# Weight splits, decay factors and the last product block in another order

## The chip, the cores and the metric

The kernel runs on one core of a Trainium2 chip (trn2). A core has TensorE (PE in the profile; its weight loads are PEld), VectorE (DVE), ScalarE (ACT), GpSimd (POOL) and SyncE (SP). Each engine runs its own list of instructions in order; semaphores make one wait for another. DMA queues are fed by SP and, for transfers that add to their target, by POOL. Times are microseconds on the device; the metric is the time of one execution, the median over runs.

## The reference, cut to what matters

One layer of a decoder for 576 tokens (512 of a prompt, 64 of eight samples), D_MODEL 1024, all in float32. One RMSNorm feeds one wide projection; its columns go to a pooling mixer, to a gated linear recurrence with four heads (HGRN) and to two branch gates. Then an output projection, a SwiGLU feed-forward with D_FF 2816, and an embedding that a gate scales:

```python
h = rms_norm(x, g_mix);  z = h @ w_in                   # 4608 columns
u, zq, zf, zi, zg, ga, gb = split(z)
pool_out = multiscale_pool(u) mixed by group
f = lb + (1 - lb) * sigmoid(zf);  k = 1 - f;  v = zi;  q = silu(zq)
o, state = hgrn2_recurrence(q, k, v, log f, state)      # in chunks, decays exp(+-cumsum(log f))
ya = pool_out @ w_pool_up;  yb = (norm(o) * silu(zg)) @ w_hgrn_up
x += (sigmoid(ga) * ya + sigmoid(gb) * yb) @ w_out
h2 = rms_norm(x, g_ffn)
x += (silu(h2 @ w_ffn_gate) * (h2 @ w_ffn_up)) @ w_ffn_down
h3 = rms_norm(x, g_ple)
x += sigmoid(h3 @ w_ple_gate) * (p @ w_ple_proj)        # gate and embedding
y = rms_norm(x, g_final)
```

## The kernel before, in words

Activations lie transposed: 128 features on the partitions, 576 tokens along the free dimension, as two halves of 288. Every weight product is made from three products of rounded parts: a matrix w is split into `whi` (w rounded to fp32r) and `wlo` (the rest), activations likewise, and TensorE adds hi·hi, lo·hi and hi·lo in one PSUM bank. In `mm` these are lines 152, 154 and 156; in `prod` they are lines 869, 870 and 871. So a block of 128 output features over 1024 inputs is 48 matmuls of 128x288.

A weight unit (128x1024, 512 KB) is loaded by SP into `raw`. There are two ways to split it. `split_piece` casts on ScalarE (line 78) and subtracts on VectorE (line 79). `split_dma` casts on ScalarE (line 86 or 90), writes the negated copy on ScalarE (line 87), and then POOL issues a DMA (line 88) that reads the weight a second time from HBM and adds it to the negated copy, which gives `wlo` without VectorE. `raw` has two buffers, `whi` and `wlo` three.

The stages, in the order of the program:

- Projections for the pooling input and HGRN. `forget` and `decays` (lines 421 to 471) make, for each head, the log gate `lt`, its running sum `gt` (a scan on VectorE), some sixty small factors `fac` on POOL, and three exponentials on ScalarE (lines 468 to 470). `scaled` (line 355) is VectorE's eviction of a product from its bank (times the norm `rn`); the banks `mm` are two in this stage. `q_in`, `q_vec` and `v_vec` prepare a head; `part1` to `part5` are its small matmuls, the first of them transposes of v (line 535) and of kS (line 540).
- `up_unit` projects both branches up. It runs just ahead of the next stage.
- The branch gates, the gate, up and most of the down projection of the feed-forward go through `pair`. A pair is two blocks of 128 outputs in Winograd's form of Strassen's scheme: seven half-sized products instead of eight. Weight parts A, B, C, D of a pair come from `p_a` (A, by `split_dma`), `p_d` (D, by `split_dma`), `p_b` and `p_hi`/`p_lo` (cast and subtract, lines 850 and 854). The bank `b` of a pair starts from a copy of bank `a`, the seed (line 979). `p_all` prepares the first pair of a run while `up_unit` still multiplies, and there `p_a` of pair 1 is prepared too.
- The last quarter of the down projection, `w_dn3`: eight blocks m of 128 outputs over 512 inputs, activations `ac` (`ahh`, `ahl`), 24 matmuls each, banks ab and cd in turn. VectorE evicts each into `res` (line 1157), ScalarE rounds and squares it (lines 240, 251), VectorE makes the low part and the sum of squares (lines 241, 252).
- The gated embedding: block m is `embed(m)` (12 matmuls with `pth`/`ptl`) and a gate (48 matmuls with `h3h`/`h3l`, line 152 again), four banks `mm` of two halves. Behind gate 0 come four matmuls (lines 268, 269) of the last norm `rms`; ScalarE's square root (line 276) reads their bank and VectorE's reciprocal (line 279) makes `rn`. `ple_vec` (lines 1171 to 1176) then evicts.

The order on each engine is set by the tile framework from the order of the source, by priorities (`tc.high_priority`) and by `tc.issue_after`. From the `up_unit` stage on, PE's order is fixed by `in_order`; before that the scheduler chooses. Weights run ahead by `ahead`: when a block takes its unit, the unit two further on is split and the one four further on is loaded.

Of the kernel before, what the change touches and what calls it, by code (L numbers as in the profile page):

```python
# [20 lines left out]
KD = 8  # L21
# [7 lines left out]
def trunk(ctx: ExitStack, tc: tile.TileContext, a, o):  # L29
# [51 lines left out]
    def split_dma(raw, u, src, hi_first=False):  # L81

        n = src.shape[-1]
        raw, hi, lo = (t[:, 0:n] for t in (raw, *u))
        if hi_first:
            nc.scalar.copy(out=hi, in_=raw)
        act(lo, raw, AF.Copy, scale=-1.0)  # L87
        nc.gpsimd.dma_start(out=lo, in_=src, accum_op=ADD)  # L88
        if not hi_first:
            nc.scalar.copy(out=hi, in_=raw)  # L90
# [21 lines left out]
    seq += [a["w_dn3"][m] for m in range(KD)] + [a["w_ple_gate"][m] for m in range(KD)]  # L112
# [3 lines left out]
    def ahead(n_raw, n_split):  # L116
# [4 lines left out]
        while state["split"] < min(n_split, state["lim"]):  # L121
            i = state["split"]

            kw = dict(pl=es_pool["fp"], tag="z", bufs=2) if i >= len(seq) - 2 else {}
            if plain0 <= i < dn0 or dn0 <= i < dn0 + KD and i % 2 or up0 + 4 <= i < out0 and i % 2:
                kw["src"] = seq[i]
            splits[i] = split(raws.pop(i), seq[i].shape[-1], **kw)
            state["split"] += 1
# [225 lines left out]
    def scaled(out, pz, rn):  # L354
        tt(out=v2(out), in0=pz[:, :, 0:HT], in1=v2(rn), op=MULT)  # L355
# [80 lines left out]
    def decays(h):  # L436
# [30 lines left out]
        nc.gpsimd.tensor_copy(out=f[:, 60:68].unsqueeze(2), in_=gt[:, TP:T].rearrange("p (b t) -> p b t", t=8)[:, :, 7:8])  # L467
        act(f, f, AF.Exp)
        act(gt, lt, AF.Exp, scale=-1.0)
        act(lt, lt, AF.Exp)  # L470
        tt(out=kt, in0=kt, in1=gt, op=MULT)
# [15 lines left out]
    def q_in(h, pz):  # L487
        zq, tq = tmpa(), tmpb()
        scaled(zq, pz, rn)
        act(tq, zq, AF.Tanh, scale=0.5)  # L490
# [213 lines left out]
    for h in range(4):  # L704
# [11 lines left out]
        if h < 2:  # L716
            decays(h + 2)
            pz = unit_mm(hx)
# [247 lines left out]
    def pair(n):  # L966
# [12 lines left out]
        seed = act(q["b"], q["a"], AF.Copy)  # L979
        q.update({t: bank(t) for t in "cd"})  # L980
# [43 lines left out]
    def p_all(n):  # L1024
# [13 lines left out]
        p_a(n + 1)  # L1038
# [106 lines left out]
    us = [next_unit() for _ in range(2)]  # L1145
    pzs = [two_banks() for _ in range(2)]
    for i in range(2):
        mm(pzs[i], us[i], ac, ks=(0, 1))
    for m in range(KD):
        if m < 2:  # L1150
            pz, u = pzs[m], us[m]
            mm(pz, u, ac, ks=(2, 3))
        else:
            pz, u = two_banks(), next_unit()
            mm(pz, u, ac)
# [48 lines left out]
    NL = 4  # L1204
    for m in range(KD - NL):
        pe_ps = embed(m)
# [73 lines left out]
def lay_out(x):  # L1280
# [30 lines left out]
    d["w_dn3"] = units(wd[2304:2816], 4)  # L1311
# [32 lines left out]
```

## Time and profile before

| What | us |
|---|---|
| median of three runs | 838.72 (838.40 to 839.03) |
| the profiled execution itself | 839.74 |
| its span, first to last instruction | 837.6 |
| PE busy | 821.8 (98%) |
| VectorE, ScalarE, GpSimd busy | 605.0 (72%), 507.8 (61%), 116.7 (14%) |
| mean granted TensorE clock | 0.995 |

In the profile a row of the timeline is an instruction: start, duration, engine, line, operation, output and inputs, and in brackets how long the engine had been idle before and who released it. A matmul's duration is modelled with its pipeline (0.29 us for 128x288), while one starts every 0.13 us; so the time that PE really loses at a wait is the distance of two starts less 0.13, some 0.16 more than the bracket says.

### The profile page before, as it was taken

What the parts mean: (1) busy time and instruction counts of PE and PEld (TensorE: products, weight loads), DVE (VectorE), ACT (ScalarE), POOL (GpSimd) and SP (SyncE); (2) the same over time, 40 slices, a digit from 0 to 9 for tenths busy, and PEclk for the clock granted to TensorE, in tenths of its full rate; (3) what the DMA queues carried; (4) which work ended last, traced back from release to release, by engine and by line L of the source; (5) the groups of instructions that cost most, each with busy time, mean ns of one, the idle gap of its engine ahead of it and who ended that gap; (6) DMA issues with size and microseconds to landing.
All of it is one profiled execution on the core that took longest, in us unless ns stands there. A gap on an engine that the chain in (4) does not pass through costs nothing.

```text
span 837.6 us, 15263 instructions
## 1 busy us (share of the span) xinstructions
PE 821.8 (98%) x6092; PEld 807.2 (96%) x6092; DVE 605.0 (72%) x996; ACT 507.8 (61%) x832; POOL 116.7 (14%) x197
## 2 busy tenths in 40 slices
PE   8999999999989999999999999999999999999996
PEld 6999899999989999999999999999999999999996
DVE  7877776764877777546978778777788767577746
ACT  7356435666777666346757767665676666565434
POOL 6304120000112110001111121112111111000000
PEclk9999999999999999999999999999999999999998
DMA  7421220322757774237757686767876568464103
GB/s 238 160 83 51 76 105 29 126 105 79 186 117 178 175 176 140 76 95 155 179 123 158 133 201 175 164 142 158 210 174 159 132 154 190 96 171 126 64 1 113
DMA packets 39766, 112.48 MB, mean 134 GB/s; under 512 B 5008, under 2 KB 9104, under 8 KB 39696
## 3 DMA queue, kind: packets, MB, share of 16 engines
q1 hardware_dynamic: 24576, 74.51, 27.6%
q0 software_dynamic: 12960, 33.82, 23.7%
q10 hardware_dynamic: 2160, 3.19, 1.0%
q8 instruction: 47, 0.77, 0.4%
q14 instruction: 23, 0.19, 0.1%
HBM read 106.50 MB, written 5.00 MB: 133 GB/s over the span
## 4 chain that ended last, share of the span: by engine, by line
PE 68%; issue 17%; POOL 4%; DMA 4%; DVE 3%; ACT 2%; SPq 0%; DVEq 0%; POOLq 0%
PE mm L154 6%; PE mm L152 6%; PE mm L156 6%; PE bb L870 3%; PE bb L869 3%; PE bb L871 3%; PE ba L871 2%; PE ba L870 2%; PE ba L869 2%; DMA wlo<-in_w_ffn_up 2%; POOL dl L88 2%; POOL wlo L88 2%; PE ba L156 1%; PE ba L152 1%; PE bb L154 1%
## 5 line engine op out<-in xcount | busy, mean ns | idle before, releaser
L78 ACT CAST whi<-raw 128x1024 fp32r<-128x1024 f32 (+2 forms) x50 | 47.0, 941 | 80.4 <-PE mm L154 38.6
L154 PE MATMUL mm<-hl,whi 128*128 128x288 f32 x320 | 70.8, 301 | 1.2 <-DVE hl L241 1.2
L152 PE MATMUL mm<-hh,whi 128*128 128x288 f32 x320 | 71.0, 304 | 1.0 <-DVE ta L355 0.9
L156 PE MATMUL mm<-hh,wlo 128*128 128x288 f32 x320 | 69.5, 299 | 0.4 <-DVE wlo L79 0.4
L79 DVE TENSOR_TENSOR wlo<-raw,whi 128x1024 fp32r<-128x1024 f32 (+2 forms) x50 | 57.1, 1143 | 14.1 <-ACT whi L78 13.3
L854 DVE TENSOR_TENSOR clo<-raw,chi 128x1024 fp32r<-128x1024 f32 (+1 forms) x38 | 43.3, 1139 | 29.3 <-ACT chi L850 29.3
L152 PEld LDWEIGHTS mm<-hh,whi 128*128 128x128 f32 x320 | 52.7, 192 | 3.8 <-ACT whi L78 1.6
L154 PEld LDWEIGHTS mm<-hl,whi 128*128 128x128 f32 x320 | 52.3, 191 | 2.5 <-DVE hl L241 1.9
L156 PEld LDWEIGHTS mm<-hh,wlo 128*128 128x128 f32 x320 | 52.3, 191 | 0.7 <-DVE wlo L79 0.6
L854 DVE TENSOR_TENSOR wlo<-rb,whi 128x1024 fp32r<-128x1024 f32 (+1 forms) x38 | 43.3, 1139 | 12.2 <-ACT whi L850 12.1
L90 ACT CAST whi<-raw 128x1024 fp32r<-128x1024 f32 (+1 forms) x38 | 37.2, 978 | 22.4 <-PE ba L870 17.8
L87 ACT ACTIVATE wlo<-raw 128x1024 fp32r<-128x1024 f32 (+2 forms) x52 | 50.6, 973 | 0.0
L850 ACT CAST chi<-raw 128x1024 fp32r<-128x1024 f32 (+1 forms) x38 | 37.0, 975 | 8.9 <-DVE raw L846 8.8
L999 ACT ACTIVATE bc<-bb 128x288 f32<-128x288 f32 x38 | 15.0, 395 | 44.5 <-PE bb L871 44.5
L850 ACT CAST whi<-rb 128x1024 fp32r<-128x1024 f32 (+1 forms) x38 | 37.3, 982 | 7.1 <-PE bb L870 3.6
L90 ACT CAST dh<-rb 128x512 fp32r<-128x512 f32 (+1 forms) x38 | 22.2, 585 | 26.0 <-PE bc L870 26.0
L840 DVE TENSOR_TENSOR rb<-rb 128x512 f32<-128x512 f32 (+1 forms) x38 | 24.6, 646 | 9.0 <-ACT dl L87 4.8
L879 DVE TENSOR_TENSOR cz<-bc,p 128x288 f32<-128x288 f32 x38 | 17.3, 455 | 16.6 <-PE bc L871 16.5
L876 DVE TENSOR_TENSOR cz<-bb,p 128x288 f32<-128x288 f32 x38 | 17.3, 456 | 16.1 <-PE bb L871 11.0
L88 POOL DMA_DIRECT2D wlo<-in_w_ffn_gate x13 | 11.1, 852 | 110.8 <-ACT wlo L87 88.0
L88 POOL DMA_DIRECT2D wlo<-in_w_dn x16 | 13.5, 847 | 87.2 <-ACT wlo L87 52.4
L845 DVE TENSOR_TENSOR raw<-raw,rb 128x512 f32<-128x512 f32 (+1 forms) x38 | 24.6, 646 | 1.0 <-ACT wlo L87 0.3
(736 smaller groups left out, 3211.8 us busy)
## 6 DMA issues: line engine op xcount, KB each, us to landing
raw<-in_w_in SPq DMA_DIRECT2D x26, 512.0 KB, 3.4
raw<-in_w_ffn_gate SPq DMA_DIRECT2D x13, 512.0 KB, 3.6
raw<-in_w_ffn_up SPq DMA_DIRECT2D x13, 512.0 KB, 4.2
wlo<-in_w_ffn_gate POOLq DMA_DIRECT2D x13, 512.0 KB, 7.0
wlo<-in_w_ffn_up POOLq DMA_DIRECT2D x13, 512.0 KB, 6.9
rb<-in_w_ffn_gate SPq DMA_DIRECT2D x9, 512.0 KB, 5.5
rb<-in_w_ffn_up SPq DMA_DIRECT2D x9, 512.0 KB, 5.5
raw<-in_w_dn SPq DMA_DIRECT2D x12, 384.0 KB, 3.7
```

Source lines behind the costliest of these rows:

```text
L78: nc.scalar.copy(out=hi[:, cs], in_=raw[:, cs])
L79: tt(out=lo[:, cs], in0=raw[:, cs], in1=hi[:, cs].bitcast(F32), op=SUB)
L87: act(lo, raw, AF.Copy, scale=-1.0)
L88: nc.gpsimd.dma_start(out=lo, in_=src, accum_op=ADD)
L90: nc.scalar.copy(out=hi, in_=raw)
L152: nc.tensor.matmul(out=out[h], lhsT=wh, rhs=xh[:, h * HT:(h + 1) * HT], start=first, stop=False)
L154: nc.tensor.matmul(out=out[h], lhsT=wh, rhs=xl[:, h * HT:(h + 1) * HT], start=False, stop=False)
L156: i = nc.tensor.matmul(out=out[h], lhsT=wl, rhs=xh[:, h * HT:(h + 1) * HT], start=False, stop=last)
L850: nc.scalar.copy(out=tiles[0][:, 0:2 * q["W"]], in_=q[raw][:, 0:2 * q["W"]])
L854: tt(out=lo, in0=q[raw][:, 0:2 * q["W"]], in1=hi.bitcast(F32), op=SUB)
L869: nc.tensor.matmul(out=out, lhsT=wh, rhs=xh, start=k == 0 and not seeded, stop=False, **kw)
L870: nc.tensor.matmul(out=out, lhsT=wh, rhs=xl, start=False, stop=False, **kw)
```

## The change

Six places:

1. `split_dma`: where the cast to `whi` is not wanted first, it is now held behind the negated copy on ScalarE. Before, the scheduler took it first in some pairs.
2. `scaled` gets a higher priority on VectorE (as if it stood 80 instructions earlier).
3. `decays` is cut in two. The exponentials and the product with `kt` become `decays2`; for heads 0 and 1 they are issued inside `q_in(0)`, after `scaled`, for heads 2 and 3 right behind `decays`, and the product is held behind the latest `scaled`.
4. The A part of pair 1 in the first run is no longer made in `p_all` by negate and accumulate; `pair(0)` makes it by a cast behind its seed and a subtraction on VectorE. One accumulating DMA of 512 KB is gone.
5. `w_dn3` is laid out as four units of 128x1024, each for two blocks, in place of eight of 128x512, and all are split by cast and subtract. Before, every second one went by negate and accumulate; four accumulating DMAs of 256 KB are gone.
6. `embed(0)` and `embed(1)` are both issued ahead of gate 0.

```diff
@@ split_dma @@
-        act(lo, raw, AF.Copy, scale=-1.0)
+        neg = act(lo, raw, AF.Copy, scale=-1.0)
         nc.gpsimd.dma_start(out=lo, in_=src, accum_op=ADD)
         if not hi_first:
-            nc.scalar.copy(out=hi, in_=raw)
+            with tc.issue_after(neg.ins):
+                nc.scalar.copy(out=hi, in_=raw)
...
-    seq += [a["w_dn3"][m] for m in range(KD)] + [a["w_ple_gate"][m] for m in range(KD)]
+    seq += [a["w_dn3"][i] for i in range(KD // 2)] + [a["w_ple_gate"][m] for m in range(KD)]
...
-            if plain0 <= i < dn0 or dn0 <= i < dn0 + KD and i % 2 or up0 + 4 <= i < out0 and i % 2:
+            if plain0 <= i < dn0 or up0 + 4 <= i < out0 and i % 2:
                 kw["src"] = seq[i]
...
     def scaled(out, pz, rn):
-        tt(out=v2(out), in0=pz[:, :, 0:HT], in1=v2(rn), op=MULT)
+        with tc.high_priority(offset=80):
+            i = tt(out=v2(out), in0=pz[:, :, 0:HT], in1=v2(rn), op=MULT)
+        state["scaled"] = i.ins
...
+    def decays2(h):
+        lt, gt, kt, f = Lt[h], Gt[h], Kt[h], fac[h]
         act(f, f, AF.Exp)
         act(gt, lt, AF.Exp, scale=-1.0)
         act(lt, lt, AF.Exp)
-        tt(out=kt, in0=kt, in1=gt, op=MULT)
+        with tc.issue_after(state["scaled"]):
+            tt(out=kt, in0=kt, in1=gt, op=MULT)
@@ q_in @@
         scaled(zq, pz, rn)
+        if not h:
+            decays2(0)
+            decays2(1)
         act(tq, zq, AF.Tanh, scale=0.5)
@@ the loop over the heads @@
             decays(h + 2)
+            decays2(h + 2)
@@ pair @@
         seed = act(q["b"], q["a"], AF.Copy)
+        if n == 0:
+            with tc.issue_after(seed.ins):
+                p_hi(nq, "A", hi_lo(), "ra")
+            p_lo(nq, "A", "ra")
@@ p_all @@
         p_load(n + 1)
-        p_a(n + 1)
+        if n:
+            p_a(n + 1)
@@ the last down blocks @@
-    us = [next_unit() for _ in range(2)]
     pzs = [two_banks() for _ in range(2)]
+    u = next_unit()
     for i in range(2):
-        mm(pzs[i], us[i], ac, ks=(0, 1))
+        mm(pzs[i], u, ac, off=512 * i, ks=(0, 1))
     for m in range(KD):
         if m < 2:
-            pz, u = pzs[m], us[m]
-            mm(pz, u, ac, ks=(2, 3))
+            pz = pzs[m]
+            mm(pz, u, ac, off=512 * m, ks=(2, 3))
         else:
-            pz, u = two_banks(), next_unit()
-            mm(pz, u, ac)
+            u = u if m % 2 else next_unit()
+            pz = two_banks()
+            mm(pz, u, ac, off=512 * (m % 2))
@@ the gated embedding @@
+    first = [embed(m) for m in range(2)]
     for m in range(KD - NL):
-        pe_ps = embed(m)
+        pe_ps = first[m] if m < 2 else embed(m)
         pg = unit_mm(hx3)
@@ lay_out @@
-    d["w_dn3"] = units(wd[2304:2816], 4)
+    d["w_dn3"] = two(wd[2304:2816])
```

What it moves, at three places. The changed file has its own line numbers: 355 is now 357, 416 is 419, 441 is 444, 445 is 448, 454 is 457, 468 to 470 are 474 to 476, 471 is 478, 490 is 500, 491 is 501, 652 is 662, 654 is 664, 850 is 861, 979 is 990.

First, VectorE at the start of the HGRN stage; `ta` is the eviction by `scaled` (of the output gate of head 0, then of its q), `gt` the scan of head 2. Before:

```order
L355 TENSOR_TENSOR ta<-mm,rn 128x576
L79 TENSOR_TENSOR wlo<-raw,whi 128x1024
L471 TENSOR_TENSOR kt<-kt,gt 128x576
L441 SCALAR_TENSOR_TENSOR gt<-cmask,lt 128x576
L471 TENSOR_TENSOR kt<-kt,gt 128x576
L416 SCALAR_TENSOR_TENSOR plo_134<-aux,C,pho_133 128x288 x2
L510 TENSOR_TENSOR kS<-kt,fac 128x512
L512 TENSOR_TENSOR kd<-kt,fac 128x96 x2
L515 TENSOR_TENSOR qk<-kt,fac 128x256
L654 SCALAR_TENSOR_TENSOR sg<-tb,ta 128x576
L445 TENSOR_TENSOR lt<-gt 128x512
L355 TENSOR_TENSOR ta<-mm,rn 128x576
```

And now:

```order
L357 TENSOR_TENSOR ta<-mm,rn 128x576
L457 SCALAR_TENSOR_TENSOR pinc<-cm_401,gt 128x16
L79 TENSOR_TENSOR wlo<-raw,whi 128x1024
L419 SCALAR_TENSOR_TENSOR plo_134<-aux,C,pho_133 128x288 x2
L444 SCALAR_TENSOR_TENSOR gt<-cmask,lt 128x576
L448 TENSOR_TENSOR lt<-gt 128x512
L457 SCALAR_TENSOR_TENSOR pinc<-cm_401,gt 128x16
L357 TENSOR_TENSOR ta<-mm,rn 128x576
L478 TENSOR_TENSOR kt<-kt,gt 128x576 x2
L664 SCALAR_TENSOR_TENSOR sg<-tb,ta 128x576
L501 SCALAR_TENSOR_TENSOR ta<-tb,ta 128x576
```

The eviction of q (the last `ta` of the first piece) came behind the `kt` products of both heads, `kS`, `kd`, `qk` and `sg`; now these stand behind it (the second `ta`). Head 2's scan stands ahead of it in both; what follows the scan, `lt` and `pinc`, now does too.

The same place on ScalarE: `fac`, `gt`, `lt` are the exponentials of a head, `tb<-ta` a tanh (of the output gate, then of q). Before:

```order
L468 ACTIVATE fac<-fac 128x68
L470 ACTIVATE lt<-lt 128x576
L469 ACTIVATE gt<-lt 128x576
L415 ACTIVATE pho_133<-aux,C 128x288
L470 ACTIVATE lt<-lt 128x576
L415 ACTIVATE pho_133<-aux,C 128x288
L652 ACTIVATE tb<-ta 128x576
L78 CAST whi<-raw 128x1024
L490 ACTIVATE tb<-ta 128x576
L469 ACTIVATE gt<-lt 128x576
L468 ACTIVATE fac<-fac 128x68
L470 ACTIVATE lt<-lt 128x576
```

And now:

```order
L662 ACTIVATE tb<-ta 128x576
L474 ACTIVATE fac<-fac 128x68
L475 ACTIVATE gt<-lt 128x576
L474 ACTIVATE fac<-fac 128x68
L476 ACTIVATE lt<-lt 128x576
L475 ACTIVATE gt<-lt 128x576
L474 ACTIVATE fac<-fac 128x68
L476 ACTIVATE lt<-lt 128x576
L475 ACTIVATE gt<-lt 128x576
L476 ACTIVATE lt<-lt 128x576
L78 CAST whi<-raw 128x1024
L500 ACTIVATE tb<-ta 128x576
```

The tanh of q stood ahead of head 2's exponentials; now it stands behind the exponentials of heads 0, 1 and 2.

Second, ScalarE at the start of the pairs; `wlo<-raw` is a negated copy (A), `dl<-rb` that of D, `bb<-ba` the seed, `pab` the last evictions of `up_unit`. Before:

```order
L850 CAST chi<-raw 128x1024
L741 COPY pab<-ba 128x288
L741 COPY pab<-bb 128x288
L87 ACTIVATE wlo<-raw 128x1024
L90 CAST whi<-raw 128x1024
L979 ACTIVATE bb<-ba 128x288
L87 ACTIVATE dl<-rb 128x512
L90 CAST dh<-rb 128x512
L883 COPY p_2949<-bd 128x288
L999 ACTIVATE bc<-bb 128x288
L90 CAST whi<-raw 128x1024
L850 CAST chi<-raw 128x1024
```

And now:

```order
L861 CAST chi<-raw 128x1024
L752 COPY pab<-ba 128x288
L752 COPY pab<-bb 128x288
L990 ACTIVATE bb<-ba 128x288
L861 CAST whi<-raw 128x1024
L87 ACTIVATE dl<-rb 128x512
L91 CAST dh<-rb 128x512
L894 COPY p_2948<-bd 128x288
L1014 ACTIVATE bc<-bb 128x288
L87 ACTIVATE wlo<-raw 128x1024
L861 CAST chi<-raw 128x1024
L91 CAST whi<-raw 128x1024
```

The negated copy and the cast of pair 1's A are gone from ahead of pair 0's seed and a cast stands behind it. In the last rows, which belong to pair 2's A and pair 1's C, the negated copy now opens the row and the cast of A closes it; before, the cast of A came first and the negated copy last, behind `chi`.

Third, PE behind gate 0, whose last rows read `h3h`; the rows with `onesr` are the norm's four matmuls, those with `pth` an embedding product. Before:

```order
L268 MATMUL mm<-sp,onesr 128x288
L269 MATMUL mm<-sp,onesr 128x288
L268 MATMUL mm<-sp,onesr 128x288
L269 MATMUL mm<-sp,onesr 128x288
L152 MATMUL mm<-pth_8759,whi 128x288 x2
L154 MATMUL mm<-ptl_8760,whi 128x288 x2
L156 MATMUL mm<-pth_8759,wlo 128x288 x2
L152 MATMUL mm<-pth_8765,whi 128x288 x2
L154 MATMUL mm<-ptl_8766,whi 128x288 x2
L156 MATMUL mm<-pth_8765,wlo 128x288 x2
L152 MATMUL mm<-h3h_8741,whi 128x288 x2
```

And now:

```order
L269 MATMUL mm<-sp,onesr 128x288
L270 MATMUL mm<-sp,onesr 128x288
L269 MATMUL mm<-sp,onesr 128x288
L270 MATMUL mm<-sp,onesr 128x288
L153 MATMUL mm<-h3h_8739,whi 128x288 x2
```

The twelve matmuls of embedding 1 are gone from between the norm's product and gate 1; they stand ahead of gate 0, behind those of embedding 0.

## The prediction

> **What bounds the kernel now.** I read the page's busy shares first, then the chain of waits, then PE's groups by line for the idle time ahead of them, then the timeline around each such wait.
>
> ```profile
> PE 821.8 (98%) x6092; PEld 807.2 (96%) x6092; DVE 605.0 (72%) x996; ACT 507.8 (61%) x832; POOL 116.7 (14%) x197
> PE 68%; issue 17%; POOL 4%; DMA 4%; DVE 3%; ACT 2%; SPq 0%; DVEq 0%; POOLq 0%
> ```
>
> PE works 98% of the span and the change takes no matmul away. So only PE's own stalls are to be had, and what any other engine saves counts only where PE waits for it. PE's timeline has six places behind the start of the program where it does (a seventh, like the fourth, is in the group):
>
> ```profile
> 83.11 0.43 PE L156 MATMUL mm<-hh,wlo 128*128 128x288 f32 x2
> 84.41 0.51 PE L152 MATMUL mm<-hh,whi 128*128 128x288 f32 x2 [0.87 <-DVE ta L355]
> ...
> 242.00 0.29 PE L871 MATMUL bd<-fs3h,wlo 128*128 128x288 f32 x1
> 243.48 0.40 PE L869 MATMUL bb<-fs0h,chi 128*128 128x288 f32 x1 [1.19 <-ACT bb L979]
> ...
> 248.49 0.30 PE L870 MATMUL ba<-fa0l,whi 128*128 128x288 f32 x1
> 249.91 0.40 PE L871 MATMUL ba<-fa0h,wlo 128*128 128x288 f32 x1 [1.13 <-DMA wlo<-in_w_in]
> ...
> 597.61 0.29 PE L870 MATMUL ba<-fa0l,whi 128*128 128x288 f32 x1
> 598.40 0.40 PE L871 MATMUL ba<-fa0h,wlo 128*128 128x288 f32 x1 [0.49 <-DMA wlo<-in_w_ffn_up]
> 598.64 0.29 PE L869 MATMUL ba<-fa1h,whi 128*128 128x288 f32 x1
> ...
> 744.91 0.30 PE L154 MATMUL bb<-ahl,whi 128*128 128x288 f32 x1
> 746.60 0.40 PE L156 MATMUL ba<-ahh,wlo 128*128 128x288 f32 x1 [1.39 <-DMA wlo<-in_w_dn]
> ...
> 763.09 0.42 PE L156 MATMUL mm<-pth,wlo 128*128 128x288 f32 x2
> 764.06 0.50 PE L152 MATMUL mm<-h3h,whi 128*128 128x288 f32 x2 [0.56 <-DVE res L1157]
> ```
>
> ```profile
> L871 PE MATMUL ba<-fa0h,wlo 128*128 128x288 f32 x26 | 8.0, 308 | 2.1 <-DMA wlo<-in_w_in 1.1 <-DMA wlo<-in_w_ffn_up 1.0
> ```
>
> A matmul starts 0.13 us after the one before (597.61 to the row it follows), so a stall costs the distance of two starts less 0.13: 1.04 (a row of x2 has its second start 0.13 later), 1.35, 1.29, 0.66, 1.56 and 0.71 us. The group gives two waits on `in_w_ffn_up` with 1.0 us of idle together, so the seventh is like the fourth, 0.65. After such a stall one more start takes 0.24 (598.40 to 598.64), 0.11 too much. Together 7.3 us, plus 0.6 for the slow second starts.
>
> **Part 1, the order in `split_dma`: -1.5 us.** At the fourth stall the late thing is the accumulating DMA, and what starts it is ScalarE's negated copy, which stood behind two casts:
>
> ```profile
> 586.78 1.05 ACT L90 CAST whi<-raw 128x1024 fp32r<-128x1024 f32 x1 [0.66 <-PE ba L870]
> ...
> 588.47 1.05 ACT L87 ACTIVATE wlo<-raw 128x1024 fp32r<-128x1024 f32 x1
> ```
>
> ```profile
> 589.82 0.86 POOL L88 DMA_DIRECT2D wlo<-in_w_ffn_up x1 [4.53 <-ACT p L883]
> ```
>
> With the negated copy first it starts at about 586.9 instead of 588.47, so the DMA, which lasts until 598.36 or so (589.82 to PE's 598.40), lands 1.5 us earlier, and 0.66 are needed. Both stalls go: 0.66 + 0.65 + 2 x 0.11. The cast of A ends where the negated copy ended, at 589.5, eight us ahead of its product; the cast between stays second, so what follows on ScalarE moves by nothing.
>
> **Parts 2 and 3, `scaled` first and `decays2`: -1.04, +0.2 us.** PE's product at 84.41 waits for a bank that VectorE empties at 83.52, behind a `kt` that waits 2.46 us for an exponential, and eight other operations:
>
> ```profile
> 79.19 0.76 DVE L471 TENSOR_TENSOR kt<-kt,gt 128x576 f32<-128x576 f32 x1 [2.46 <-ACT gt L469]
> ...
> 83.52 0.75 DVE L355 TENSOR_TENSOR ta<-mm,rn 128x576 f32<-128x576 f32 x1
> ...
> 89.19 0.75 DVE L355 TENSOR_TENSOR ta<-mm,rn 128x576 f32<-128x576 f32 x1
> ```
>
> ```profile
> 84.30 0.69 ACT L490 ACTIVATE tb<-ta 128x576 f32<-128x576 f32 x1 [2.28 <-DVE ta L355]
> ...
> 88.42 0.26 ACT L468 ACTIVATE fac<-fac 128x68 f32<-128x68 f32 x1
> ```
>
> ```profile
> 90.87 0.60 PE L535 MATMUL aux<-ident,ta 128*128 128x128 f32 x4
> ```
>
> The product whose bank it is ended near 77; in the new order the eviction follows head 2's scan and runs near 78, five us ahead of need. The stall goes. What is late next is the transposes at 90.87, which read v's eviction (89.19 to 89.94, a margin of 0.9) and which PE now reaches 1.04 earlier, at 89.83. From q's tanh to v's eviction VectorE had 4.9 us of work (84.30 to 89.19); in the new order `kt` and `pinc` leave that stretch and `kS`, `kd`, `k2` enter it, about as much. The tanh stands behind nine exponentials, of which the third head's `fac` needs POOL's factors; I work those out at 80 (VectorE's `pinc`, on which POOL waited, now comes near 77.5), so the tanh starts near 83, v is out at 88.7 and the margin holds. Bounds: nothing back, or all of the 1.04; I take 0.2, near the first, since a margin of a few tenths is all that is left at several small matmuls of this stage. The later heads' order on PE changes too (it is the scheduler's there); no row prices that, and it stands in a rival.
>
> **Part 4, pair 1's A: -2.85, +0.3 us.** Ahead of pair 0's seed stood two ScalarE operations that waited for `up_unit` to free their buffers:
>
> ```profile
> 241.12 1.07 ACT L87 ACTIVATE wlo<-raw 128x1024 fp32r<-128x1024 f32 x1
> 242.08 1.04 ACT L90 CAST whi<-raw 128x1024 fp32r<-128x1024 f32 x1
> 243.01 0.41 ACT L979 ACTIVATE bb<-ba 128x288 f32<-128x288 f32 x1
> ...
> 248.25 1.04 ACT L90 CAST whi<-raw 128x1024 fp32r<-128x1024 f32 x1 [2.49 <-DMA raw<-in_w_in]
> ...
> 252.04 0.39 ACT L979 ACTIVATE bb<-ba 128x288 f32<-128x288 f32 x1
> ```
>
> ```profile
> 241.93 9.93 SPq L70 DMA_DIRECT2D raw<-in_w_in x2
> ```
>
> ```profile
> raw<-in_w_in SPq DMA_DIRECT2D x26, 512.0 KB, 3.4
> ```
>
> Without them the seed runs at 241.1 to 241.5, ahead of PE's 242.13: 1.35 + 0.11 gone. The A part now comes from a cast at 241.6 to 242.6 and a subtraction of 1.2 us, ready by 244; PE wants it at 247, so the DMA stall (1.29 + 0.10) goes too. What hides the two new operations is ScalarE's idle 2.49 us and VectorE's slack there; uncovered they would cost 2.3. Next late: pair 1's own seed (252.04 to 252.43). Its five ScalarE operations start when `raw` of pair 2 lands (248.25). PE reads that seed 36 matmuls after 248.36, at 254.5 before and now at 251.65. If `raw` lands as before, 0.9 us come back. It took 6.3 us (241.93 to 248.25) beside the accumulating DMA that is gone, against 3.4 for the median one; with 3.4 nothing comes back. I take 0.3.
>
> **Part 5, double units: -1.66, +0.2 us.** The stall at 746.60 is a DMA that no longer exists; the four casts and subtractions are done long before. 1.56 + 0.10 go. ScalarE has fewer operations, VectorE in the blocks themselves about as many as before (one subtraction of 1.2 for two of 0.7). The next late thing is VectorE's last eviction:
>
> ```profile
> 749.38 0.46 DVE L1157 TENSOR_TENSOR res<-ba,res 128x288 f32<-128x288 f32 x1 [1.95 <-PE ba L156]
> ...
> 755.17 0.82 DVE L241 SCALAR_TENSOR_TENSOR h3l<-res,C,h3h 128x576 fp32r<-128x576 f32 x1 [0.84 <-ACT h3h L240]
> ...
> 763.46 0.45 DVE L1157 TENSOR_TENSOR res<-bb,res 128x288 f32<-128x288 f32 x1
> ```
>
> VectorE had 2.8 us idle in these blocks and none from 755.17 to that eviction. PE comes 1.66 earlier, VectorE, with its rows' durations added up in the new order, some 1.4, so the wait of 0.71 for the eviction at 763.46 grows to about 0.9. Bounds: hidden (-0.71), or VectorE only 0.7 earlier (+1.0); I take +0.2.
>
> **Part 6, embedding 1 ahead of gate 0: +1.24 us.** It does not cover that wait. In the built program embedding 1 gets the bank pair of the last down block, so it is embedding 1 itself that waits for the same eviction, in place of gate 0. And it leaves the place where it covered another wait:
>
> ```profile
> 770.47 1.05 ACT L78 CAST whi<-raw 128x1024 fp32r<-128x1024 f32 x1 [3.31 <-PE mm L154]
> 771.42 0.74 ACT L276 ACTIVATE rn<-mm,eps 128x576 f32<-128x576 f32 x1
> ```
>
> ```profile
> 771.07 0.43 PE L152 MATMUL mm<-pth,whi 128*128 128x288 f32 x2
> ```
>
> Gate 1 takes the bank of the norm's product, which ScalarE's square root reads until 772.16, itself behind a cast that waits for gate 0. Embedding 1's twelve matmuls filled 771.07 to 772.66. Without them PE stands from 771.07 to 772.16 plus the 0.15 that a release takes (763.91 to 764.06): 1.24. Queued behind the waiting gate 1 is all of PE's rest. Bounds: 0 if the square root came ahead of its cast, 1.59 if the release were as late as embedding 1's end.
>
> **The sum**, on the profiled execution's own 839.74 us (span 837.6): -1.52 - 1.04 + 0.2 - 2.85 + 0.3 - 1.66 + 0.2 + 1.24 = -5.1, so 834.6. That execution lay 1.0 above the median of 838.72; against the median it is 833.6.
>
> One term belongs to no part:
>
> ```profile
> 133.00:140.00 7.00, 7.00 (x44) 6.72 (x43) 6.20 (x12) 3.92 (x8) 0.00 (x0) 0.76 0.00 0
> ```
>
> In this window the granted clock averages 0.76, in the middle of the small matmuls of the heads; (1 - 0.76) x 7.00 = 1.7 us at most are lost there. A shifted program may lose that again, twice, or not at all. I leave it as it is, with 1.7 to either side in the range. The Trainium skill, "TensorE: Matmul & The Clock Gate", section "Part 1: The HAM clock gate", says that the clock is halved after an idle window of about 3.4 us and that these windows run free of the program. By that rule the loss is a matter of phase and either outcome is as likely after as before; the row agrees so far that a 0.76 over 7 us is 3.4 us at half.
>
> **Rivals.**
>
> A, 0.12: the embeddings do what their place promises: no wait of gate 1, and the last eviction covered. For it: ScalarE has 3.31 us of idle time ahead of 770.47. Against: the cast and the square root follow gate 0 in order. -5.1 - 1.24 - 0.91 = -7.3: 831.4.
>
> B, 0.16: the heads pay. `scaled` now stands ahead of the state updates on VectorE, and each of heads 1 to 3 loses one eviction (0.75, the row at 89.19) on PE. For it: the small matmuls of these heads read what VectorE has just written. Against: VectorE is idle 2.46 us and more in this stage. +2.25: 835.9.
>
> C, 0.05, slower: the tanh of q stands behind head 2's `fac`. If POOL's factors come when they came before, that exponential runs at 88.42, three more and a cast (0.6 x 3 + 1.0) put the tanh at 91.4, v's eviction ends 5.6 later at 97.0, and PE waits at its transposes from 89.83: 7.3. -5.1 - 0.2 + 7.3 = +2.0: 840.7. It makes the kernel slower from `fac` at 86.5 on. Against: their order on VectorE puts `pinc` eight us earlier (it stood behind the evictions).
>
> **How the numbers follow.** My forecast has 0.65, A 0.12, B 0.16, C 0.05, 0.02 something unseen. The likeliest's own range is 832.2 (-7.07 - 0.71 + 1.24) to 836.2 (-7.07 + 1.04 + 0.9 + 1.0 + 1.59). The clock's 1.7 and rivals A and B widen it to 831.0 to 837.3. What a measurement can tell from no change is about 0.2%, 1.7 us: faster is below 837.0, slower above 840.4. Faster: the forecast, A and most of B, 0.88; same: a bit of each with the clock against it, 0.07; slower: C, 0.05.
>
> **What would show it.** Right: no PE idle time on `ta` near 84, on the seed near 242, on a `wlo` DMA near 248, 598, 699 and 745; PE waiting for `res` in a row that reads `pth`, and in gate 1's first row for `rn`, over 1 us. Wrong: gate 1 without a wait (A), PE idle at small matmuls from 90 to 190 (B), tanh of q later than 86 (C), or a wait for pair 1's seed near 252 over 0.9 us.

## The result, and the profile after

The change makes the kernel slower: 844.27 us (843.65 to 846.17, four runs) against 838.88 (838.40 to 840.10, four runs), a ratio of 1.0066 with a 95% interval of 1.0046 to 1.0085. The forecast was 833.6. The profiled execution took 844.43 us, its span 842.6 against 837.6 before: +5.0.

The page of the changed kernel: busy shares, the granted clock in 40 slices of 21 us, and the chain that ended last.

```profile
PE 825.3 (98%) x6092; PEld 810.2 (96%) x6092; DVE 607.4 (72%) x997; ACT 502.9 (60%) x823; POOL 115.2 (14%) x192
...
PEclk9999799999999999999999999999999999999999
...
PE 92%; DVE 2%; ACT 2%; POOL 2%; DMA 1%; issue 1%; SPq 0%; DVEq 0%; ACTq 0%
```

PE still fills the span, with the same 6092 matmuls, but 3.5 us busier, and one slice of the clock, the fifth (84 to 105 us), stands at 7. So part of the loss is not idle time but slower matmuls, and the largest part of both lies in one place. (Line numbers have moved: `mm` is now 153, 155 and 157, `prod` 880 to 882, the tanh of q 500, the exponentials 474 to 476, v's eviction 357.)

Most of the forecast came true. PE's groups and its timeline show the stalls of before, and what is left of them:

```profile
L882 PE MATMUL ba<-fa0h,wlo 128*128 128x288 f32 x26 | 7.7, 295 | 0.0
```

```profile
767.60 0.53 PE L153 MATMUL mm<-pth,whi 128*128 128x288 f32 x2 [0.58 <-DVE res L1174]
...
776.08 0.29 PE L270 MATMUL mm<-sp,onesr 128*128 128x288 f32 x1
777.35 0.53 PE L153 MATMUL mm<-h3h,whi 128*128 128x288 f32 x2 [0.98 <-ACT rn L277]
```

The first row is the group that had idled 2.1 us for `wlo` DMAs; it idles 0.0. The stalls at 84.41, 243.48 and 746.60 have no successor in the timeline either. At the end, embedding product 1 waits for the last eviction and gate 1 for the norm, both foretold.

Most of what was not foretold lies between 90 and 105 us, in head 0 of HGRN. First PE:

```profile
90.52 0.63 PE L545 MATMUL aux<-ident,ta 128*128 128x128 f32 x4 [0.32 <-DVE ta L357]
90.98 0.60 PE L550 MATMUL aux<-ident,kS 128*128 128x128 f32 x4
93.56 0.31 PE L556 MATMUL aux<-ident,v 128*96 128x128 f32 x1 [1.98 <-POOL v L537]
...
94.24 0.33 PE L565 MATMUL aux<-lt,kt 128*64 128x64 f32 x2
97.43 1.01 PE L574 MATMUL aux<-qc,kt 128*128 128x192 f32 x2 [2.86 <-ACT vn L547]
```

By distances of starts, as in the prediction (these small matmuls start 0.11 us apart), these are stalls of 0.49, 2.14 and 2.93 us, 5.6 together, for three different engines. Then the clock. Three windows of the changed kernel:

```profile
97.40:105.20 7.80, 7.77 (x23) 5.08 (x24) 4.19 (x9) 3.11 (x10) 0.00 (x0) 0.52 0.22 67
114.50:119.00 4.50, 4.50 (x23) 4.46 (x23) 3.39 (x11) 0.16 (x1) 0.00 (x0) 0.62 0.36 128
169.00:174.00 5.00, 5.00 (x27) 4.96 (x27) 5.00 (x9) 1.91 (x5) 0.00 (x0) 0.66 0.33 105
```

and the only such window of the kernel before:

```profile
136.50:139.90 3.40, 3.40 (x15) 3.31 (x15) 2.84 (x8) 1.35 (x3) 0.00 (x0) 0.50 0.00 0
```

The granted clock is the third figure from the right. (1 - 0.52) x 7.80 = 3.7 us are lost in the first, 1.7 in each of the other two: 7.1 us, against 1.7 before. The first stretch of half clock in fact begins at 94.60, behind the second stall; up to 97.43 PE stands idle in it, and what it loses there is in the stall already.

| Where | us, after less before |
|---|---|
| six stalls and their twin, with the slow second starts (7.3, less the one kept at the end, and 0.5) | -7.1 |
| the waits of embedding product 1 and gate 1, with their slow second starts, less the wait of 0.71 before | +1.3 |
| three stalls in head 0 | +5.6 |
| half clock | +5.4 |
| sum | +5.2 |
| the two spans | +5.0 |

Now why the three engines were late. ScalarE, VectorE and POOL, of the changed kernel:

```profile
81.98 0.26 ACT L474 ACTIVATE fac<-fac 128x68 f32<-128x68 f32 x1 [2.41 <-POOL fac L463]
...
84.01 1.03 ACT L78 CAST whi<-raw 128x1024 fp32r<-128x1024 f32 x1
84.94 0.68 ACT L500 ACTIVATE tb<-ta 128x576 f32<-128x576 f32 x1
85.53 1.04 ACT L78 CAST whi<-raw 128x1024 fp32r<-128x1024 f32 x1
95.84 1.04 ACT L78 CAST whi<-raw 128x1024 fp32r<-128x1024 f32 x1 [9.28 <-DMA raw<-in_w_in]
96.80 0.58 ACT L547 COPY vn<-aux 128x512 f32<-128x512 f32 x1
```

```profile
85.66 0.76 DVE L501 SCALAR_TENSOR_TENSOR ta<-tb,ta 128x576 f32<-128x576 f32 x1 [4.63 <-ACT tb L500]
...
89.62 0.75 DVE L357 TENSOR_TENSOR ta<-mm,rn 128x576 f32<-128x576 f32 x1
90.29 1.22 DVE L79 TENSOR_TENSOR wlo<-raw,whi 128x1024 fp32r<-128x1024 f32 x1
91.42 0.75 DVE L478 TENSOR_TENSOR kt<-kt,gt 128x576 f32<-128x576 f32 x1
92.09 1.22 DVE L79 TENSOR_TENSOR wlo<-raw,whi 128x1024 fp32r<-128x1024 f32 x1
93.22 0.75 DVE L357 TENSOR_TENSOR ta<-mm,rn 128x576 f32<-128x576 f32 x1
```

```profile
90.44 3.07 POOL L537 COPY v<-ta 128x192 f32<-128x192 f32 x1 [8.49 <-DVE ta L357]
```

Read them in this order. ScalarE waits 2.41 us for POOL's factors of head 2, runs the exponentials and a cast, and gets to q's tanh at 84.94. VectorE stands idle 4.63 us for that tanh. Behind the waiting operation stands all of VectorE's row: q's scale, the small products, v's eviction and, behind that, the weight subtraction at 90.29. That subtraction is what frees a `raw` buffer, so the next weight load starts late. The rows of the tile `raw` from 84 to 97 us give the load's start, before and after:

```profile
L70 SPq DMA_DIRECT2D raw<-in_w_in x3: 327/327/327, 85.4 to 93.3; - x3
```

```profile
L70 SPq DMA_DIRECT2D raw<-in_w_in x2: 328/328/328, 91.6 to 93.3; - x2
```

The first load of the stretch is issued at 91.6 instead of 85.4. ScalarE's cast of it stands in ScalarE's row ahead of `vn`, the copy of the first transposes, and waits 9.28 us; `vn`, whose data PE had made by 91.15, is copied at 96.80, and PE waits for it. In the kernel before, a cast stood ahead of `vn` too, but the subtraction had come early, its buffer was loaded from 85.4 on, and PE did not wait; POOL's copy took 0.34 us:

```profile
84.19 1.21 DVE L79 TENSOR_TENSOR wlo<-raw,whi 128x1024 fp32r<-128x1024 f32 x1
```

```profile
90.80 1.05 ACT L78 CAST whi<-raw 128x1024 fp32r<-128x1024 f32 x1 [0.60 <-PE mm L154]
91.75 0.58 ACT L537 COPY vn<-aux 128x512 f32<-128x512 f32 x1
```

```profile
90.00 0.34 POOL L527 COPY v<-ta 128x192 f32<-128x192 f32 x1 [1.62 <-DVE ta L355]
```

So one late tanh on one engine reaches PE through VectorE's row, a buffer, a DMA and ScalarE's row.

### The profile page after: what moved, and what is told of

Its sections match the earlier page's. It is cut to its first block, busy times and chain, and to the rows that moved or that the text cites. A ratio compares the mean times of both kernels' runs of the same rounds, so it can differ in the third digit from the quotient of the medians.

```text
span 842.6 us, 15160 instructions
## 1 busy us (share of the span) xinstructions
PE 825.3 (98%) x6092; PEld 810.2 (96%) x6092; DVE 607.4 (72%) x997; ACT 502.9 (60%) x823; POOL 115.2 (14%) x192
## 4 chain that ended last, share of the span: by engine, by line
PE 92%; DVE 2%; ACT 2%; POOL 2%; DMA 1%; issue 1%; SPq 0%; DVEq 0%; ACTq 0%
PE bb L881 7%; PE bb L880 7%; PE bb L882 7%; PE mm L153 6%; PE mm L155 6%; PE mm L157 6%; PE ba L882 4%; PE ba L881 4%; PE ba L880 4%; PE bd L882 2%; PE bd L881 2%; PE bd L880 2%; PE bc L881 2%; PE bc L880 2%; PE bc L882 2%; PE ba L153 2%
## 5 line engine op out<-in xcount | busy, mean ns | idle before, releaser
L78 ACT CAST whi<-raw 128x1024 fp32r<-128x1024 f32 (+2 forms) x50 | 48.8, 975 | 92.4 <-PE mm L155 32.5
L79 DVE TENSOR_TENSOR wlo<-raw,whi 128x1024 fp32r<-128x1024 f32 (+2 forms) x50 | 59.2, 1183 | 20.4 <-ACT whi L78 19.4
L87 ACT ACTIVATE wlo<-raw 128x1024 fp32r<-128x1024 f32 (+1 forms) x47 | 47.1, 1002 | 24.2 <-PE ba L882 21.6
L87 ACT ACTIVATE dl<-rb 128x512 fp32r<-128x512 f32 (+1 forms) x38 | 22.7, 598 | 29.5 <-PE bc L882 28.9
L857 DVE TENSOR_TENSOR raw<-raw 128x512 f32<-128x512 f32 (+1 forms) x38 | 24.6, 646 | 0.8
```

The lines of the kernel that those rows point to most:

```text
L78: nc.scalar.copy(out=hi[:, cs], in_=raw[:, cs])
L79: tt(out=lo[:, cs], in0=raw[:, cs], in1=hi[:, cs].bitcast(F32), op=SUB)
L87: neg = act(lo, raw, AF.Copy, scale=-1.0)
```

## The experiments

Names: before is the kernel before, the change is the kernel with all six parts. All ratios are to runs of the kernel before on the same chip; three chips were used, so two ratios from different chips compare less closely. Each kernel has line numbers of its own.

| Kernel | Ratio to before | 95% | Stalls of PE at head 0, us |
|---|---|---|---|
| the change | 1.0066 | 1.0046 to 1.0085 | 0.49 + 2.14 + 2.93 |
| parts 2, 3 undone | 0.9950 | 0.9930 to 0.9969 | 1.08, at 84.15 |
| parts 2, 3 alone | 1.0094 | 1.0068 to 1.0119 | 0.52 + 2.14 + 3.20 |
| tanh first | 0.9963 | 0.9942 to 0.9984 | 2.38 |
| v's copy on VectorE | 1.0030 | 1.0006 to 1.0053 | 0.50 + 0.31 + 4.14 |
| part 3 undone, part 2 kept | 0.9950 | 0.9928 to 0.9971 | 1.17, at 84.22 |
| part 2 undone, part 3 kept | 1.0021 | 0.9995 to 1.0047 | 1.60 + 1.00 + 1.18 |
| cast held behind vn | 0.9997 | 0.9969 to 1.0026 | 0.47 + 2.14 |
| tanh first and cast held | 0.9934 | 0.9913 to 0.9955 | none |
| the same, repeated | 0.9949 | 0.9933 to 0.9965 | none |
| the same with part 6 undone | 0.9921 | 0.9904 to 0.9938 | none |
| and banks in the other order | 0.9921 | 0.9899 to 0.9943 | none |

### Are the heads the cause: parts 2 and 3 undone, and alone

The change with the old `scaled` and the old `decays` (shown shortened):

```diff
     def scaled(out, pz, rn):
-        with tc.high_priority(offset=80):
-            i = tt(out=v2(out), in0=pz[:, :, 0:HT], in1=v2(rn), op=MULT)
-        state["scaled"] = i.ins
+        tt(out=v2(out), in0=pz[:, :, 0:HT], in1=v2(rn), op=MULT)
...
-    def decays2(h):
-        lt, gt, kt, f = Lt[h], Gt[h], Kt[h], fac[h]
         act(f, f, AF.Exp)
...
-        if not h:
-            decays2(0)
-            decays2(1)
...
-            decays2(h + 2)
```

> Parts 2 and 3 (scaled first, decays2) undone; parts 1, 4, 5, 6 stay. Theory H (all of the loss comes from parts 2 and 3 at head 0, the other parts gave what was forecast): -1.5 (part 1), -2.85 (part 4), -1.66 + 0.03 (part 5), +1.14 + 0.11 (part 6, as the trace after shows it) = -4.7 against before, so about 834.1; PE's stall at 84.4 is back, none from 90 to 98. Rival K (the clock's windows wander with any shift of the program and make the loss): between 834 and 838, with half-clock windows in other places than before.

And the kernel before with these two parts alone (the same lines the other way round):

> The kernel before with parts 2 and 3 alone. Theory H: it carries the whole loss, 838.9 + (844.3 - 834.1) = 849, with the three stalls of 0.5, 2.1 and 2.9 us between 90 and 98 and half clock behind them. Rival K: 839 to 845.

Measured: 0.9950 without them (-0.50%, -4.2 us of 838.9) and 1.0094 with them alone (+7.9 us). The two add up to +3.7, with about 2 us of uncertainty on each; the whole is +5.4. So parts 1, 4, 5 and 6 gain, within that uncertainty, what they were forecast to gain (-1.52 - 2.85 + 0.3 - 1.66 + 0.2 + 1.24 = -4.3), and parts 2 and 3 lose more than that. The time without them, 834.7 by the ratio, fits both theories; what decides is the kernel with the two parts alone. K put it at 845 at most and H at 849; it took 846.8 by the ratio, and its trace has the three stalls in the same place with half clock behind them.

### Which of the two parts

One kernel with part 3 undone (the decays whole again, the priority of `scaled` kept), one with part 2 undone (`scaled` without priority, `decays2` kept). The diffs are the halves of the one above.

> The change with its part 3 undone (one function for the decays again, at its old place); part 2, the higher priority of the evictions, stays. On VectorE the rows around q's eviction then stand as in the kernel before, and on ScalarE the tanh of q stands ahead of head 2's exponentials again. Theory T, the place of the exponentials ahead of the tanh makes the loss: it behaves like the kernel with both parts undone, 0.3 to 0.7 per cent faster than the kernel before, with the 1.0 us stall near 84.4 back and none at 90 to 98. Rival S, the priority of the evictions makes the loss by putting v's eviction ahead of the weight subtraction: slower than before by 0.3 to 1 per cent.

> The change with its part 2 undone (the evictions at their ordinary priority); part 3, the split of the decays, stays. ScalarE's row is that of the change; on VectorE the first weight subtraction stands ahead of v's eviction. Theory T: the tanh is as late as in the change (near 85), so q's scale and all behind it too; 0.3 to 0.9 per cent slower than before, with a wait for the late weight piece near 97 that is at most 1.2 us shorter (the eviction and subtraction that change places take 0.7 and 1.1 us), and the wait for v's eviction near 90 longer by as much. Rival S: 0.2 to 0.6 per cent faster than before.

With part 2 alone the tanh stands where it stood before:

```profile
84.11 0.69 ACT L493 ACTIVATE tb<-ta 128x576 f32<-128x576 f32 x1 [2.28 <-DVE ta L357]
...
91.56 0.58 ACT L540 COPY vn<-aux 128x512 f32<-128x512 f32 x1
```

and the kernel is 0.50% faster than before, just as with both undone: the priority by itself does nothing that the time shows. With part 3 alone the first weight subtraction comes ahead of v's eviction again, and the tanh stays late:

```profile
84.59 0.68 ACT L499 ACTIVATE tb<-ta 128x576 f32<-128x576 f32 x1
...
93.75 1.04 ACT L78 CAST whi<-raw 128x1024 fp32r<-128x1024 f32 x1 [7.53 <-DMA raw<-in_w_in]
94.70 0.58 ACT L546 COPY vn<-aux 128x512 f32<-128x512 f32 x1
```

It comes out at 1.0021, just below what was expected and hardly told from no change. The stalls sum to 3.8 us instead of 5.6: the load is earlier by the subtraction's place, v's eviction later by it. So part 3 makes the loss, and part 2, which puts that eviction ahead of the subtraction, adds to it when the two stand together.

### The tanh itself

The change, with head 2's exponentials held behind the tanh of head 0's q:

```diff
-        act(f, f, AF.Exp)
-        act(gt, lt, AF.Exp, scale=-1.0)
-        act(lt, lt, AF.Exp)
+        with tc.issue_after(state["tq"]) if h == 2 else nullcontext():
+            act(f, f, AF.Exp)
+            act(gt, lt, AF.Exp, scale=-1.0)
+            act(lt, lt, AF.Exp)
...
-        act(tq, zq, AF.Tanh, scale=0.5)
+        state["tq"] = act(tq, zq, AF.Tanh, scale=0.5).ins
```

> The changed kernel, with the exponentials of head 2 held behind the tanh of head 0's q (three ScalarE operations moved, nothing else). Theory T (the tanh is late because it waits behind head 2's exponentials and these for POOL; everything from 90 to 98 follows from it): the tanh starts near 80.5 instead of 84.9, v is evicted near 86, the next weight's subtraction and its buffer come four us earlier, no stall from 90 to 98 and none at 84, no half clock at 97: about 844.3 - 5.6 - 3.9 = 834.8, or 833 if the extra half-clock window at 170 goes too. Rival P (POOL's copy of v, 3.07 us beside a busy VectorE, is the cause by itself): some 2 us of stall stay, 837 to 840.

```profile
80.40 0.68 ACT L501 ACTIVATE tb<-ta 128x576 f32<-128x576 f32 x1
...
91.82 1.04 ACT L78 CAST whi<-raw 128x1024 fp32r<-128x1024 f32 x1 [7.98 <-DMA raw<-in_w_in]
92.77 0.58 ACT L548 COPY vn<-aux 128x512 f32<-128x512 f32 x1
```

```profile
85.89 3.08 POOL L538 COPY v<-ta 128x192 f32<-128x192 f32 x1 [4.68 <-DVE ta L357]
```

0.9963, faster than before. The tanh runs 4.5 us earlier, v's eviction too, and the first two stalls are gone, though POOL's copy of v lasts as long as in the change: it now ends at 88.97, before PE wants it. One stall of 2.38 us is left, at the copy `vn` behind the waiting cast. The load that this cast waits for was issued at 87.0 instead of 91.6 and took 4.7 us to land. The time fell between the two expectations, for that stall and the clock behind it. The stall also tells two errors apart: here the tanh runs earlier than the 83 of the forecast, and PE still waits for `vn`.

### POOL's copy of v

The change, with the copy that took 3.07 us on POOL given to VectorE (`nc.gpsimd.tensor_copy` becomes `nc.vector.tensor_copy` in `v_vec`).

> The changed kernel, with head copies of v made by VectorE instead of POOL. Rival P: the wait of 2.1 us goes and with it part of the half clock, 840 to 842. Theory T: the copy is done near 92 instead of 93.5, but PE's next wait, for ScalarE's copy vn that stands behind a weight cast, which stands behind a load, ends at 97.4 as before; the time stays within 0.5 of 844.3, the wait of 2.9 grows by what the other loses.

1.0030, or 841.4, which is within P's 840 to 842; but the stalls do what T said. The stall for v shrinks from 2.14 to 0.31 us, but the one for `vn` grows from 2.93 to 4.14, since `vn` hangs on the cast and the cast on its load (95.21 here, 95.84 in the change). Two stalls with different causes stood one behind the other; removing the first moves most of its time into the second. The three fell by 0.6 us together. The profiled execution also lost 2.0 us less to the clock (5.1 against 7.1), so the time does not price the copy by itself.

### The cast ahead of the copies

One instruction moved: the cast that waits for the late load is held behind the copies of the transposes. In the change, and in the kernel with the tanh first (shown shortened):

```diff
-        ahead(i + 5, i + 3)
+        with tc.issue_after(state["vn"]) if i == state["hold"] else nullcontext():
+            ahead(i + 5, i + 3)
...
-        nc.scalar.copy(out=vn, in_=pv)
+        state["vn"] = nc.scalar.copy(out=vn, in_=pv).ins
...
+        if h == 1:
+            state["hold"] = state["use"]
         q_in(h, unit_mm(hx))
```

> The change with one ScalarE instruction moved: the weight cast that waits for the late raw load (95.84 us in the change's trace) is held behind the copies of head 0's transposes (vn, kn, t, vk) instead of ahead of them. Nothing else in the heads moves; the tanh is as late as before. Theory Q, the 2.93 us stall at 97.43 is that cast standing in ScalarE's order: the stall goes, and with it some of the half clock behind it (7.8 us at 0.52, so up to 3.7 us): 2.9 to 6.6 us less than the change, which is 0.3 per cent slower to 0.15 per cent faster than the kernel before. Rival B, the copies are late for another reason (VectorE's rows or the POOL copy of v): the stall comes back at the next product, at most 1 us is won, still 0.5 per cent or more slower than before.

> Head 2's exponentials behind the tanh of q (as in the run with the tanh first) and the cast held behind the copies of the transposes. That run had one stall left, 2.38 us at 93.41, and a clock of 0.72 in 98 to 108 us and 0.84 in 84 to 98 behind it (about 5 us together). Theory Q: the stall goes and most of the half clock with it: 0.6 to 1.0 per cent faster than the kernel before, the fastest so far. Rival B: the stall comes back at a later copy: 0.2 to 0.45 per cent faster, as with the tanh first alone. A third way, H: the stall goes but the clock halves all the same in the small products of the head: 0.45 to 0.65 per cent.

In the change, with the tanh as late as ever, `vn` is copied at once and PE's third stall is gone:

```profile
90.90 0.58 ACT L548 COPY vn<-aux 128x512 f32<-128x512 f32 x1 [4.62 <-PE aux L546]
```

```profile
93.96 0.33 PE L566 MATMUL aux<-lt,kt 128*64 128x64 f32 x2
94.22 0.97 PE L575 MATMUL aux<-qc,kt 128*128 128x192 f32 x2
```

That gives 0.9997 against 1.0066, as expected by Q: 0.7%, 5.8 us by the ratios, 3.1 us between the two spans (842.6 and 839.5). The half clock behind the second stall stayed:

```profile
94.20:104.60 10.40, 10.40 (x35) 7.60 (x34) 6.10 (x14) 4.22 (x12) 0.00 (x0) 0.51 0.29 100
```

PE works through all of it, so it costs 5.1 us here, 1.4 more than in the change, where the third stall covered its beginning. The ratio says more than the spans in part because two of the ten executions, by their clock, ran without this loss; the last section comes back to them.

With both, the stage runs without a stall. PE at the place where the change stood, and the clock there:

```profile
90.40 0.27 PE L558 MATMUL aux<-ident,v 128*96 128x128 f32 x1
...
91.04 0.33 PE L567 MATMUL aux<-lt,kt 128*64 128x64 f32 x2
91.30 0.59 PE L576 MATMUL aux<-qc,kt 128*128 128x192 f32 x2
```

```profile
84.00:98.00 14.00, 14.00 (x97) 12.36 (x96) 12.27 (x23) 5.52 (x15) 3.08 (x1) 1.00 0.29 95
98.00:108.00 10.00, 10.00 (x68) 9.72 (x67) 5.85 (x14) 2.10 (x4) 0.00 (x0) 0.85 0.26 87
```

0.9934, and 0.9949 when repeated, which misses the 0.55 to 0.85 per cent that were expected of the repeat. 838.88 x 0.9934 = 833.3 (834.6 by the repeat), and the span is 831.8 against 837.6: -5.8, where the forecast's sum for the change was -5.1. Two places in ScalarE's order, head 2's exponentials and one cast, separate the change from the time that was forecast for it.

### The end of the program

Part 6 undone on top of that (product 1 between gate 0 and gate 1 again), then also the banks of the last down blocks swapped from the third block on, so that gate 0 need not wait for the last eviction:

```diff
-    first = [embed(m) for m in range(2)]
...
-        pe_ps = first[m] if m < 2 else embed(m)
+        pe_ps = embed(m)
```

```diff
             u = u if m % 2 else next_unit()
+            if m == 2:
+                banks.reverse()
```

> The kernel with the tanh first and the cast held, with part 6 undone as well: embedding product 0, gate 0, embedding product 1, gate 1, on the double units of the last down blocks. That kernel's trace has two waits there, 0.742 us at 756.90 (embedding product 1 on the last down block's eviction) and 1.146 us at 766.50 (gate 1 on the norm's last instruction). Theory E, part 6 costs its forecast: the second goes, since embedding product 1 runs while the norm is made; the first stays, in front of gate 0 instead: 1.1 us or 0.14 per cent less than the repeat beside it, 0.7 to 0.9 per cent faster than before. Rival N: the norm takes longer here and the second stays: the same as the repeat beside it.

> The same, and the last down blocks take their PSUM banks in the other order from the third block on, so that gate 0 reuses banks that have long been read and embedding product 0 takes those of the last block. Theory E: the wait on the last eviction stands ahead of embedding product 0 and is no shorter there (the same eviction, one product earlier in the order): within 0.1 per cent of the run beside it, at most 0.7 us better or worse. Rival G: the wait is between the last matmul and the first product on its banks, and moves with them to where nothing else stands to cover it: 1.0 to 1.7 us slower than the run beside it, since one product (1.6 us) less lies between.

> The kernel with the tanh first and the cast held once more, on the same chip as the two beside it: 0.55 to 0.85 per cent faster than before again; the two others are compared with it.

Without part 6 gate 1 has no wait, and the one for the last eviction is ahead of gate 0:

```profile
757.04 0.51 PE L154 MATMUL mm<-h3h,whi 128*128 128x288 f32 x2 [0.67 <-DVE res L1178]
```

0.9921 against 0.9949 of the repeat beside it, 2.4 us between the medians (833.28 and 835.70) and 1.8 between the spans; the rows account for 1.1 (1.14 gone, the other wait 0.83 instead of 0.74). Another 0.6 of the 1.8 is there when embedding product 0 starts (754.61 against 755.20), ahead of which the two kernels have the same order, so it is no effect of part 6. Part 6 costs about what was forecast. With the other bank order the wait is 0.58 us, ahead of embedding product 0: not worse, as rival G had it. The ratio is 0.9921 again; the median is 0.95 us and the span 2.2 us longer than beside it, of which one more window of half clock is 1.7 (two against one), so the time shows no gain. These two have the lowest ratios of the study, 0.8% below the kernel before, though their intervals overlap with that of 0.9934; 0.9921 / 1.0066 = 0.986, 1.4% below the change.

## Why the prediction was wrong, point by point

**What bounds the kernel, and parts 1, 4, 5 and 6** held. PE's stalls at 243, 249, 598, 699 and 746 us are gone. Part 4's 0.3 for pair 1's seed was not needed: PE's timeline has no wait there. Part 5's wait grew to 0.74, where 0.9 was forecast. Part 6's is 1.14, where 1.24 was forecast. Together, with parts 2 and 3 undone, -4.2 us measured (-5.9 to -2.6 by the interval) and -4.3 forecast. Rival A fell with the two waits at the end.

**Parts 2 and 3** are where it failed, and the sentence is "the tanh starts near 83, v is out at 88.7 and the margin holds". The stall at 84.41 went as forecast. Three things were wrong behind it. The second is the step that failed; the first made it worse, and the third was put at nothing.

- The size. POOL's factors were put at 80, and the exponential that waits for them ran at 81.98. `pinc` came at 77.79, near the 77.5 of the forecast, but POOL's operations behind it dragged on to 81.95: three that had taken 0.19 to 0.20 us each in the kernel before, while VectorE was idle, took 0.71 to 0.81 beside a busy VectorE. From there to the tanh it took 3.0 us, as in the forecast. The tanh came at 84.94, v's eviction ended at 90.37 instead of 88.7. This alone cost 0.49 us.
- The followers. For every wait one has to name what is queued behind it, and the working stopped at v's eviction. Behind it stood, in the new order, the weight subtraction, which had been at 84.19; behind that a `raw` buffer, a load and a cast, and in ScalarE's row behind the cast the copy `vn`. This cost 2.93 us, and 2.38 were left with the tanh ahead of its forecast time, so it does not hang on the late factors. It could be seen in the order of the instructions: on VectorE the subtraction had moved behind the scale that waits for the tanh and behind v's eviction, and on ScalarE the cast stood ahead of the copy, with the wait for a load that the subtraction releases.
- The company. In the kernel before, the copy of v fell into a gap of VectorE; in the change VectorE works back to back after its idle wait, and the copy took 3.07 us. This cost 2.14 us.

**The clock** was given 1.7 us to either side. It cost 5.4, of which 3.7 came straight behind the stalls: the term was not independent of the others, as the range had it. All four executions of the change have a mean granted clock of 0.987 to 0.990; the 69 of the kernel before that ran beside the experiments have 0.991 to 0.998.

**The rivals.** C named the right place and the right mechanism, the tanh behind head 2's exponentials, with a chance of 0.05, and priced it by one follower only: it "makes the kernel slower from `fac` at 86.5 on". It made it slower at 81.98, with a tanh at 84.94, so that C's own sign, a tanh later than 86, did not show. Head 2's exponentials first cost more than all the rest gains even without the late factors that C supposed; holding them back is worth 1.0066 against 0.9963. B's sign, PE idle at small matmuls between 90 and 190 us, was seen, but in head 0 and for C's reason.

## What to carry to other kernels

When an edit puts an instruction of engine A ahead of one that engine B waits for, list everything that stands behind B's waiting instruction up to the next idle time, and follow each buffer that these free, to its load and to the engine that takes the load in order: the dearest follower here was three hand-overs away. Look for instructions that wait for a load and stand in an in-order row ahead of copies that TensorE needs; moving one such cast was worth 0.7% in the change, and 0.1 to 0.3% with the tanh first. A forecast for several edits is best split into pieces that can be run alone, since one small one can eat the gain of all the others, as here.

## What the runs showed of the hardware

**POOL beside VectorE.** The copy of v, 128x192, took 0.34 us in the kernel before and 3.07 and 3.08 us in the change and with the tanh first. In the change it began at 90.44 and ended at 93.51, just behind three VectorE operations back to back with both inputs in SBUF (the two subtractions and `kt`, 90.29 to 93.31); the eviction from PSUM that follows at 93.22 did not hold it. VectorE made the same copy in 0.25 us. The Trainium skill, "SBUF — State Buffer", section "SBUF: two separate sides", says that VectorE operations with two SBUF inputs and GpSimd operations that read SBUF lock each other out for a whole instruction. The rows agree, and add that a run of such operations keeps the copy out for longer than one of them: 3.07 us is three. With part 2 undone it began at 91.22 beside two of them and took 1.94.

**The clock behind a stall.** In the profiles of all six kernels whose stalls at head 0 come to 2.4 us or more together, the clock is halved in or behind them, from 93.4 to 96.9 us on: for 10.2 us in five of them, for 6.8 with part 2 undone. The one with a single stall of 2.38 us, which ends at 93.41:

```profile
93.40:103.80 10.40, 10.39 (x33) 7.61 (x34) 6.12 (x14) 3.77 (x12) 0.00 (x0) 0.51 0.15 50
```

The kernels with no stall there, or one of 1.0 to 1.2 us, lost at most about 1.7 us to the clock from 84 to 120 us. So in that profiled execution a stall of 2.4 us costs 7.5: itself and (1 - 0.51) x 10.4 = 5.1. The Trainium skill, "TensorE: Matmul & The Clock Gate", section "Part 1: The HAM clock gate", asks for an idle window of about 3.4 us; here 2.38 us, among matmuls of 64 to 192 columns, were enough.

But the half clock does not come every time. The mean clock of each execution is on record. Of the ten with the cast held, eight have 0.988 to 0.992 and took 840.5 to 843.5 us; two have 0.998 and took 835.0 and 835.1. These two left no trace, but it is the same program, so its stalls of 0.47 and 2.14 us were probably there. The difference of 5.4 to 8.5 us is about what the profiled execution, one of the eight, lost to half clock: 5.1 at head 0 and 1.7 in a later window. One of the ten executions with part 2 undone is of that kind too (0.998, 835.8 us; the other nine 841.3 or more). So a stall here makes half clock likely, not certain, and the medians of such kernels depend on how often it came.

**Half clock without a stall.** All profiles but one also have one or two windows of 3.4 us at half clock somewhere between 105 and 194 us, with PE busy: at 136.5 in the kernel before, and in the two profiles of the kernel without stalls once here:

```profile
105.00:108.60 3.60, 3.60 (x16) 3.50 (x16) 3.60 (x12) 0.21 (x1) 0.00 (x0) 0.53 0.52 168
```

and once here:

```profile
182.40:186.00 3.60, 3.60 (x17) 3.51 (x17) 2.72 (x7) 2.28 (x6) 0.00 (x0) 0.53 0.00 0
```

(1 - 0.53) x 3.6 = 1.7 us each. So the place of one such loss can change between two executions of one program, and it is no sign of a kernel. Chance may not be all of it: the change and the kernel with parts 2 and 3 alone have their two windows at the same places, from 115.0 and from 169.6 on. What sets them off is open. All stretches of half clock from 84 to 240 us in the thirteen profiles last 3.4 us, or two or three times that (6.8, 10.2).
